# A two-block transformer kernel on one core: ordering the same instructions by a simulated timeline instead of the scheduler's default rule

## Chip, cores and metric

The kernel runs on one core of a Trainium2 chip. The metric is the device time of one execution in microseconds (us); lower is better. TensorE multiplies matrices, VectorE (DVE), ScalarE (ACT) and GpSimd (POOL) do the elementwise work, SyncE (SP) issues most of the transfers. Each of them works through its own queue of instructions and waits for others by semaphores.

## The reference

Two transformer blocks of 256 tokens with a model width of 1024 run behind one another, all in float32.

```python
def first_block(x, ...):
    h = x
    h = h + moba_attention(rms_norm(h, norm_mix[0]), ...)
    h = h + conv_ffn(rms_norm(h, norm_ffn[0]), ...)
    h = h + rwkv7_time_mix(rms_norm(h, norm_mix[1]), ...)
    h = h + conv_ffn(rms_norm(h, norm_ffn[1]), ...)
    return rms_norm(h, norm_final)

def second_block(x, mem, ...):
    mem_k, mem_v = jnp.split(mem @ mem_w_kv, 2, axis=-1)
    for i in range(2):
        mix = differential_attention(h, ...) if i == 0 else dsa_sparse_mla(h, ...)
        h = layer_norm(alpha * h + mix, ...)
        h = layer_norm(alpha * h + memory_cross_attention(h, mem_k, mem_v, ...), ...)
        h = layer_norm(alpha * h + hierarchical_moe(h, ...), ...)
    return h
```

The listing is shortened: the loop over the layers of the first block is written out, and arguments are left out. The time mix is a linear recurrence over the tokens with a state of 64 x 64 per head (16 heads). The sparse attention scores all keys with a small indexer, keeps the 64 best of each query (top-k) and attends to those alone. The layer of experts has 16 experts of width 512 and gives each token to two of them.

## The kernel before, in words

The stages run one after the other, in the order of `build`: moba attention, feed-forward, time mix, feed-forward, then twice an attention (differential, then sparse), memory attention and experts. Tokens stand in two tiles of 128. Activations are transposed (`to_T`, matmuls with an identity at L246) so that features lie on the partitions. A weight is loaded as float32 over SP's queue (`load`, L170) and split into a high and a low part: `wh` is a cast on ACT (L191), `wl = w - wh` a subtraction on VectorE, in places on POOL (L192). A product is then three matmuls, high by high, low by high and high by low (`mm3`, L215 to L217).

Two PSUM pools hold results: one of four tiles for short-lived products (`mm`, `pp`) and one of four for running sums (`acc`); some stages open further ones (`rkp`, `va`). A stage's instructions are recorded in program order, with some stages recorded as interleaved pieces: while the time mix works on its chunks, pieces of the memory projection (the tile `va`, keys and values of the memory attention) are recorded between its steps.

After the recording, the framework's scheduler puts each engine's instructions into the queue that the engine will work through. It keeps the data dependencies, hands out the buffers of the pools, and where several instructions of one engine could come next, its rule decides. No transfer, tile size, engine or pool is set there: only the order, and with it which buffer of a pool a tile gets. It is set up at L2005, by the `TileContext` around `build`.

The lines that the prediction's steps speak of:

- Norms: L276 adds the sums to the residual, L277 squares on ACT, L279 is a power on POOL, L282 the scaled rows on VectorE, L246 their transposes on TensorE. L352 to L369 are the layer norm.
- Moba attention: L475 and L476 scores of a head, L494 the scaled softmax on VectorE, L504 its transposes, L509 and L510 the product with the values.
- Time mix, mixes: L637 computes the mixed inputs on VectorE, L641 and L642 split them. L1161 to L1184 compute rotation angles for the second block on VectorE; they are independent of the time mix.
- Time mix, heads: the receptance and key projections write `rkp`; L730, L756, L770, L773, L790 and L801 prepare a group of four heads.
- Time mix, recurrence: L848 to L881 invert small triangular matrices, L911 to L966 run the chunks of 64 tokens: L929 reads the state `S`, L933 adds on VectorE, L940 gives `UV`, L952 and L958 the new state, L966 the output. Each chunk needs the state of the chunk before. L987 to L1013 normalise the output and transpose it (L1009); the output projection (`acc`) needs that.
- Sparse attention: L1834 and L1835 are the indexer's scores, one head of 16 at a time; L1837 a relu on ACT, L1841 and L1843 their weighted sum on VectorE. The top-k is a serial chain on VectorE: eight rounds of maximum and replacement (L1849, L1850). L1866 and L1874 project keys and values, L1884 are the attention scores, L1885 to L1893 the softmax, which needs the top-k's mask, L1736 its transposes, L1906 and L1907 the product with the values.
- Experts: L1612 and L1614 gather tokens, L1639 the gate and up products, L1645 the gated product on VectorE, L1654 its transposes, L1668 the down product, L1625 scatters the result back.

The top-k chain and its input, in the code:

```python
for rd in range(8):
    for t, cs in ((0, slice(0, 128)), (1, slice(128, 384))):
        vec.max(mx[:, t], sc[:, cs])
        vec.match_replace(sc[:, cs], mx[:, t], sc[:, cs], low)
```

Of the kernel before, what the change touches and what calls it, by code (L numbers as in the profile page):

```python
# [53 lines left out]


class MoeQueue:
    """Weight chunks of a memory attention and a MoE layer in the order of use: slots of a ring, and some filled only once."""

    def __init__(self, nc, wq, wo, wg, wu, wd):
        self.nc, self.ring, self.free, self.loaded, self.used = nc, [], [], [], 0  # L60
# [1948 lines left out]
```

## Time and profile before

| | before |
|---|---|
| median of three runs | 1748.44 us (1744.04, 1748.44, 1748.51) |
| span of the profiled execution | 1741.2 us |
| mean granted clock of TensorE | 0.958 of full speed |
| TensorE busy | 1619.0 us, 93% |
| VectorE busy | 888.9 us, 51% |
| ScalarE busy | 699.2 us, 40% |
| GpSimd busy | 186.8 us, 11% |
| data moved | 375.39 MB, 216 GB/s on average |

The span reaches from the first to the last instruction of one profiled execution; no other time of that execution is given. A run's time lies some microseconds above it. A busy share is an average over stages with different limits, so the prediction reads single stages. In the timeline the stages lie as follows (us from the start of the span): moba attention 0 to 147, feed-forward to 341, time mix to 650 (its mixes 350 to 397, its heads to 485), feed-forward to 845, differential attention to 970, memory attention to 1046, experts to 1297, sparse attention to 1406, memory attention to 1480, experts to the end.

A row of a timeline gives the start, the duration, the engine, the line, the operation with what it writes and reads, and how many such instructions stand in a row; a bracket gives the idle time before and what ended it. Matmuls are pipelined, so their durations overlap and the distance of two starts is the pace.

### The profile page before, as it was taken

What the parts mean: (1) busy time and instruction counts of PE and PEld (TensorE: products, weight loads), DVE (VectorE), ACT (ScalarE), POOL (GpSimd) and SP (SyncE); (2) the same over time, 40 slices, a digit from 0 to 9 for tenths busy, and PEclk for the clock granted to TensorE, in tenths of its full rate; (3) what the DMA queues carried; (4) which work ended last, traced back from release to release, by engine and by line L of the source; (5) the groups of instructions that cost most, each with busy time, mean ns of one, the idle gap of its engine ahead of it and who ended that gap; (6) DMA issues with size and microseconds to landing.
All of it is one profiled execution on the core that took longest, in us unless ns stands there. A gap on an engine that the chain in (4) does not pass through costs nothing. (4 is left out here: it accounts for less than half of the span.)

```text
span 1741.2 us, 26063 instructions
## 1 busy us (share of the span) xinstructions
PE 1619.0 (93%) x10383; PEld 1213.0 (70%) x10383; DVE 888.9 (51%) x1864; ACT 699.2 (40%) x1288; POOL 186.8 (11%) x153
## 2 busy tenths in 40 slices
PE   7899999879899999999999899999979989999995
PEld 6778999758788778999887785444427778544532
DVE  3567655498857567665568643111126964311112
ACT  5676455345434546554467432010116643201101
POOL 4610000056623110000101000000000000000000
PEclk9999999989969998999999899999989999999998
DMA  9324653432321329643661948999948177899983
GB/s 346 134 97 148 216 187 129 125 106 85 97 69 58 108 81 308 206 159 121 226 233 49 339 173 330 387 387 387 386 146 284 74 254 258 325 387 386 387 321 127
DMA packets 230353, 375.39 MB, mean 216 GB/s; under 512 B 17092, under 2 KB 105932, under 8 KB 230220
## 3 DMA queue, kind: packets, MB, share of 16 engines
q1 hardware_dynamic: 215616, 359.88, 58.7%
q10 hardware_dynamic: 14604, 13.71, 2.6%
q8 instruction: 86, 1.41, 0.3%
q14 instruction: 47, 0.39, 0.1%
HBM read 372.52 MB, written 1.05 MB: 215 GB/s over the span
## 5 line engine op out<-in xcount | busy, mean ns | idle before, releaser
L191 ACT CAST wh<-w 128x1024 fp32r<-128x1024 f32 (+1 forms) x253 | 260.3, 1039 | 232.5 <-PE mm L216 123.1
L192 DVE TENSOR_TENSOR wl<-w,wh 128x1024 fp32r<-128x1024 f32 (+1 forms) x214 | 257.1, 1210 | 151.9 <-ACT wh L191 151.4
L1639 PE MATMUL mm<-mw,xg 128*64 128x512 f32 x1024 | 230.2, 594 | 0.0
L217 PE MATMUL mm<-xh,wl 128*128 128x256 f32 x800 | 227.1, 284 | 0.0
L216 PE MATMUL mm<-xl,wh 128*128 128x256 f32 x800 | 226.9, 284 | 0.0
L215 PE MATMUL mm<-xh,wh 128*128 128x256 f32 x800 | 226.6, 283 | 0.0
L1639 PEld LDWEIGHTS mm<-mw,xg 128*64 128x64 f32 x1024 | 73.7, 137 | 144.0 <-issue 142.5
L215 PEld LDWEIGHTS mm<-xh,wh 128*128 128x128 f32 x800 | 151.9, 190 | 1.9
L216 PEld LDWEIGHTS mm<-xl,wh 128*128 128x128 f32 x800 | 151.3, 189 | 2.3 <-DVE xl L252 0.3
L217 PEld LDWEIGHTS mm<-xh,wl 128*128 128x128 f32 x800 | 151.5, 189 | 0.0
L1668 PE MATMUL mm<-mw,hT 128*64 128x512 f32 x512 | 118.7, 596 | 1.7 <-issue 1.7
L215 PE MATMUL acc<-wh,xh 128*128 128x512 f32 x284 | 112.9, 403 | 1.6 <-ACT xh L249 0.9
L216 PE MATMUL acc<-wl,xh 128*128 128x512 f32 x284 | 114.0, 402 | 0.0
L217 PE MATMUL acc<-wh,xl 128*128 128x512 f32 x284 | 113.3, 401 | 0.0
L192 POOL TENSOR_TENSOR wl<-w,wh 128x1024 fp32r<-128x1024 f32 x39 | 93.4, 2404 | 79.4 <-ACT wh L191 73.9
L1645 DVE TENSOR_TENSOR hid<-hid,mm 128x512 f32<-128x512 f32 x16 | 11.0, 687 | 168.3 <-PE mm L1639 168.3
L1668 PEld LDWEIGHTS mm<-mw,hT 128*64 128x64 f32 x512 | 36.6, 137 | 69.2 <-issue 67.5
L1675 DVE SCALAR_TENSOR_TENSOR Y<-mm,cs,Y 128x512 fp32r<-128x512 f32 x32 | 24.0, 751 | 114.2 <-ACT Y L1674 114.2
L1674 ACT ACTIVATE Y<-mm,cs 128x512 fp32r<-128x512 f32 x32 | 22.0, 687 | 146.8 <-PE mm L1668 146.8
L215 PE MATMUL acc<-wh,fh 128*128 128x512 f32 x176 | 69.5, 395 | 0.0
L217 PE MATMUL acc<-wh,fl 128*128 128x512 f32 x176 | 69.5, 396 | 0.0
L216 PE MATMUL acc<-wl,fh 128*128 128x512 f32 x176 | 69.3, 394 | 0.0
(529 smaller groups left out, 3127.8 us busy)
## 6 DMA issues: line engine op xcount, KB each, us to landing
mw<-in_moe_w_gate_dram SPq DMA_DIRECT2D x61, 1024.0 KB, 14.2
mw<-in_moe_w_up_dram SPq DMA_DIRECT2D x60, 1024.0 KB, 14.3
mw<-in_moe_w_down_dram SPq DMA_DIRECT2D x57, 1024.0 KB, 14.1
w<-in_ffn_w_gate_dram SPq DMA_DIRECT2D x22, 1024.0 KB, 5.9
w<-in_ffn_w_up_dram SPq DMA_DIRECT2D x22, 1024.0 KB, 6.7
w<-in_ffn_w_down_dram SPq DMA_DIRECT2D x22, 1024.0 KB, 6.3
w<-in_attn_w_qkv_dram SPq DMA_DIRECT2D x12, 1024.0 KB, 10.8
w<-in_a_w_in_dram SPq DMA_DIRECT2D x12, 1024.0 KB, 10.6
```

The costliest lines, as they stand in the source:

```text
L191: nc.scalar.copy(r[0], raw)
L192: (lo_eng or nc.vector).tensor_tensor(r[1], raw, r[0], op=ALU.subtract)
L215: mm(out, lhs[0], rhs[0], start=start, stop=False)
L216: mm(out, lhs[0], rhs[1], start=False, stop=False)
L217: mm(out, lhs[1], rhs[0], start=False, stop=stop)
L1639: mm(ps[64 * e:64 * e + 64], xg[:, k, e * 64:e * 64 + 64], mq.slab(w[2 * (k // 4) + e], k % 4), start=k == 0, stop=k == 7)
L1645: tt(hid, hid, gu[1], op=ALU.mult)
L1668: mm(pd[hf][64 * e:64 * e + 64], hT[:, k, 64 * e:64 * e + 64], mq.slab(w[2 * hf + e], k), start=k == 0, stop=k == 3)
L1674: act.activation(y[0], pd[hf], AF.Copy, scale=cs)
L1675: vec.scalar_tensor_tensor(y[1], pd[hf], cs, y[0], op0=ALU.mult, op1=ALU.subtract)
```

## The change

```diff
@@ kernel(**inputs)
     out = nc.dram_tensor("out_0_dram", (1, S, D), F32, kind="ExternalOutput").ap()
-    with tile.TileContext(nc) as tc:
+    with tile.TileContext(nc, schedule_with_timeline_sim=True) as tc:
         build(tc, aps, out[0])
```

The framework's scheduler orders the instructions by a timeline that it simulates instead of by its default rule. A docstring of a class goes as well, which leaves the line numbers as they are. The instructions of each engine are the same ones; their order in each queue differs, and with it the assignment of buffers. In the two feed-forward layers the order on TensorE stays the same. Three places at which it differs:

POOL, at the start of the time mix (rms is the norm's scale, L192 the subtraction for a weight's low part, aT a constant that is cleared, xvl and xl low parts of the mixes). Before:

```order
L279 TENSOR_TENSOR rms<-rms,mhalf 128x1 x2
L824 MEMSET aT 128x256
L825 MEMSET aT 128x16
L279 TENSOR_TENSOR rms<-rms,mhalf 128x1 x2
L192 TENSOR_TENSOR wl<-w,wh 128x1024
L642 TENSOR_TENSOR xvl<-xm,xvh 128x256
L642 TENSOR_TENSOR xl<-xm,xh 128x256 x2
```

With the change:

```order
L279 TENSOR_TENSOR rms<-rms,mhalf 128x1 x2
L192 TENSOR_TENSOR wl<-w,wh 128x1024
L824 MEMSET aT 128x256
L279 TENSOR_TENSOR rms<-rms,mhalf 128x1
L825 MEMSET aT 128x16
L279 TENSOR_TENSOR rms<-rms,mhalf 128x1
L642 TENSOR_TENSOR xvl<-xm,xvh 128x256
L642 TENSOR_TENSOR xl<-xm,xh 128x256 x2
```

The subtraction moved ahead of the last two powers of the norm; before, it stood behind them.

TensorE, the end of the chunks' second half in the time mix (L929 reads the state, L940 makes UV, L966 the output, L1009 transposes the normalised output, va is the memory projection, acc the output projection). Before:

```order
L215 MATMUL va<-wh,xh 128x512
L216 MATMUL va<-wl,xh 128x512
L217 MATMUL va<-wh,xl 128x512
L940 MATMUL mm<-Z,A 64x64
L215 MATMUL va<-wh,xh 128x512
L1009 MATMUL mm<-c_ident,Y 128x128 x3
L940 MATMUL mm<-Z,A 64x64 x7
L1009 MATMUL mm<-c_ident,Y 128x128
L1013 MATMUL mm<-tg,g_5252 128x128 x4
L966 MATMUL mm<-UV,A 64x64 x8
L216 MATMUL va<-wl,xh 128x512
L217 MATMUL va<-wh,xl 128x512
```

With the change:

```order
L952 MATMUL mm<-UV,BK 64x64 x8
L966 MATMUL mm<-UV,A 64x64 x8
L929 MATMUL mm<-S,AR 128x64 x8
L940 MATMUL mm<-Z,A 64x64
L1009 MATMUL mm<-c_ident,Y 128x128 x4
L940 MATMUL mm<-Z,A 64x64 x7
L1013 MATMUL mm<-tg,g_5252 128x128 x4
L966 MATMUL mm<-UV,A 64x64 x8
L215 MATMUL acc<-wh,xh 128x512
L216 MATMUL acc<-wl,xh 128x512
L215 MATMUL acc<-wh,xh 128x512
L216 MATMUL acc<-wl,xh 128x512
```

The memory projections between the steps of the chain, and behind L966, have moved to places further ahead; behind L966 now twelve matmuls of the output projection stand before the next L1009.

TensorE, sparse attention, from the key projection (L1866) and the value projection (L1874) to the attention scores (L1884); before, all rows of L1834 and L1835 stand ahead of this piece. Before:

```order
L215 MATMUL acc<-cqh,wh 96x256
L216 MATMUL acc<-cql,wh 96x256
L217 MATMUL acc<-cqh,wl 96x256
L1866 MATMUL acc<-ckvT,w 96x256 x16
L1874 MATMUL acc<-w,ckvT 128x512 x8
L1884 MATMUL acc<-kT,qT 128x128
L1884 MATMUL acc<-kT,qT 128x256
```

With the change (the 16 matmuls of L1866 and five of the eight of L1874 stand ahead of this piece):

```order
L1834 MATMUL mm<-kiz,qiT 128x128
L1835 MATMUL mm<-kiz,qiT 128x256
L1834 MATMUL mm<-kiz,qiT 128x128
L1835 MATMUL mm<-kiz,qiT 128x256
L1874 MATMUL acc<-w,ckvT 128x512 x3
L1834 MATMUL mm<-kiz,qiT 128x128
L1835 MATMUL mm<-kiz,qiT 128x256
L1834 MATMUL mm<-kiz,qiT 128x128
L1835 MATMUL mm<-kiz,qiT 128x256
L1884 MATMUL acc<-kT,qT 128x128
L1884 MATMUL acc<-kT,qT 128x256
```

The indexer's scores moved back behind most of the projections, so that the last two heads of them stand directly ahead of L1884.

## Rows read from the trace of the kernel before

**Rows 1.** Page, busy time: busy us, share of the span, instructions.

```profile
PE 1619.0 (93%) x10383; PEld 1213.0 (70%) x10383; DVE 888.9 (51%) x1864; ACT 699.2 (40%) x1288; POOL 186.8 (11%) x153
```

**Rows 2.** TensorE's waits: line, released by; us in all, times, longest.

```profile
PE mm L246 <- DVE nrm L282: 20.2, 8, 9.2
...
PE mm L504 <- DVE s L494: 6.4, 3, 3.8
...
PE pp L801 <- DVE rn L758: 5.0, 3, 2.8
PE mm L1654 <- DVE hid L1645: 4.3, 7, 0.8
...
PE mm L929 <- DVE S L958: 2.5, 1, 2.5
```

**Rows 3.** TensorE's timeline, moba attention: start us, us, engine, line, work, count [idle before].

```profile
54.09 0.28 PE L216 MATMUL acc<-xl,wh 128*128 128x256 f32 x1
54.21 0.28 PE L217 MATMUL acc<-xh,wl 128*128 128x256 f32 x1
...
59.11 0.30 PE L504 MATMUL mm<-c_ident,s 128*128 128x128 f32 x1 [3.76 <-DVE s L494]
...
61.59 0.41 PE L216 MATMUL acc<-xl,wh 128*128 128x256 f32 x1
61.80 0.41 PE L217 MATMUL acc<-xh,wl 128*128 128x256 f32 x1
```

**Rows 4.** POOL's timeline at the start of the time mix.

```profile
353.74 2.63 POOL L192 TENSOR_TENSOR wl<-w,wh 128x1024 fp32r<-128x1024 f32 x1 [5.40 <-DMA vraw<-in_rwkv_w_rkv_dram]
```

**Rows 5.** Busy time by window, mixes of the time mix: window, its us, each engine's busy us.

```profile
348.24:391.77 43.53, 34.33 (x134) 22.73 (x134) 43.36 (x72) 17.78 (x34) 24.62 (x23) 0.90 0.35 106
```

**Rows 6.** VectorE's timeline, mixes of the time mix.

```profile
352.49 5.03 DVE L637 SCALAR_TENSOR_TENSOR xm<-xx,par,x 128x256 f32<-128x256 f32 x6
...
390.75 3.41 DVE L637 SCALAR_TENSOR_TENSOR xm<-xx,par,x 128x256 f32<-128x256 f32 x6
...
394.48 0.61 DVE L1173 TENSOR_SCALAR angk<-anga 128x48 f32<-128x48 f32 x1
...
398.46 0.21 DVE L1184 SCALAR_TENSOR_TENSOR anga<-angy,anga 128x48 f32<-128x48 f32 x1
```

**Rows 7.** TensorE's timeline, heads of the time mix.

```profile
473.46 0.90 PE L790 MATMUL mm<-c_ident,bk 128*128 128x128 f32 x3 [2.19 <-DVE bk L781]
```

**Rows 8.** Busy time by window of line L872: PE, PEld, granted clock, DMA share.

```profile
486.90:517.70 30.80, 3.82 (x64) 3.56 (x64) 0.50 0.19 59
575.70:600.00 24.30, 1.20 (x64) 1.09 (x64) 1.00 0.36 118
```

**Rows 9.** TensorE's timeline, chunks of the time mix, second half.

```profile
595.09 1.11 PE L929 MATMUL mm<-S,AR 64*128 64x64 f32 x16
...
617.88 1.15 PE L966 MATMUL mm<-UV,A 128*64 128x64 f32 x16
...
628.16 0.66 PE L1009 MATMUL mm<-c_ident,Y 128*128 128x128 f32 x4 [1.02 <-DVE Y L1004]
```

**Rows 10.** Busy time by window of tile va: first PE with its count.

```profile
595.00:614.00 19.00, 9.69 (x34) 5.80 (x35) 0.00 (x0) 1.17 (x2) 1.00 0.26 85
617.00:628.50 11.50, 5.63 (x23) 4.24 (x23) 0.00 (x0) 1.17 (x2) 1.00 0.32 97
```

**Rows 11.** TensorE's timeline, sparse attention.

```profile
1352.96 0.60 PE L1835 MATMUL mm<-kiz,qiT 128*128 128x256 f32 x2
...
1369.69 4.75 PE L1884 MATMUL acc<-kT,qT 128*128 128x128 f32 x28
1374.73 1.36 PE L1736 MATMUL mm<-c_ident,s 128*128 128x128 f32 x6 [0.29 <-DVE s L1893]
```

**Rows 12.** VectorE's timeline, sparse attention.

```profile
1360.81 0.61 DVE L1849 MAX8 mx<-sc 128x8 f32<-128x128 f32 x2
...
1374.39 0.55 DVE L1893 TENSOR_SCALAR s<-s,st 128x128 f32<-128x128 f32 x2
```

## The prediction

> **What bounds the kernel now.** I read the page's busy shares and slices first, then TensorE's waits, then the timelines of the places where the order changes. TensorE is busy for 1619.0 us of the span of 1741.2 [rows 1]: whatever an order can win or lose on this engine is idle time and clock. By the table of its waits, the largest are the norms between layers (L246 waits 20.2 us for the scaled rows of L282, in eight places), and behind them waits of matmuls that stand too early in the queue: L504 6.4 us in three, L801 5.0 in three, L929 2.5 in one, L1654 4.3 in seven [rows 2]. Each stops the whole engine, since the matmuls behind it in the queue, ready or not, come after it. The timeline shows it: the transposes L504 stand directly behind their own scores, TensorE stops for 3.76 us, and 1.1 us later it runs at the half clock; there a 256-column matmul starts every 0.21 us instead of every 0.12 [rows 3]. A stretch of 3.4 us at the half clock so costs about 3.4 x (1 - 0.12/0.21) = 1.5 us.
>
> The change has the same instructions on the same engines; only each engine's own order differs. So the rule of the sum is: a matmul moved back behind ready ones removes its wait; ready matmuls used up early are missing later, where a chain over VectorE has nothing beside it; and work moved ahead on VectorE or POOL delays what is behind it.
>
> **The change part by part.**
> 1. Moba attention (the stretch around [rows 3]): L475, L504 and L509 go behind 10 to 40 more projection matmuls. What that can remove is 6.4 us of waits [rows 2] and two half-clock stretches of 1.5 each, 9.4 in all. The projections used early are missing for the last heads, beside the output projection: one wait like the longest, 3.8 us, and a stretch of 1.5 come back. Bounds -9.4 and 0; I take **-4**.
> 2. Start of the time mix: on POOL the subtraction L192, 2.63 us [rows 4], now stands ahead of both L279, the powers of the rms norm, for which TensorE's transposes wait. On SP, one weight load (L170) goes ahead of loads of the value projection, on ACT two casts (L191) ahead of the squares (L277). TensorE has nothing else there. Bounds 0 (the weight is there before the norm begins) and +5 (the load as well is late); **+2.6**, the subtraction itself.
> 3. Mixes of the time mix: VectorE is busy 43.36 of 43.53 us [rows 5], so its work is the path. The rope angles (L1161 to L1184, thirteen instructions, which stand behind the last mix L637 and take from 394.48 to 398.46 [rows 6]) are pulled in between the mixes. Bounds 0 and +3.9; **+2**. The same rows show a reverse effect: six mixes take 5.03 us while that POOL subtraction runs, and 3.41 later [rows 4, 6]; since it moves ahead, up to 1.6 us could come back here, and that lies in the bounds. The Trainium skill (page "SBUF — State Buffer", section on the two separate sides) says that VectorE with two SBUF inputs and GpSimd lock each other out of a shared port for a whole instruction. By that rule all of the 1.6 comes back and this sum would be 1.6 lower; the trace agrees in direction (5.03 against 3.41), though shorter POOL operations run beside the later mixes too.
> 4. Heads of the time mix (rkp projections between L730 and L801): L756, L770, L790 and L801 go behind 10 to 20 more projections. Waits of 5.0 for L801 [rows 2] and 2.2 for L790 [rows 7], with three half-clock stretches of 1.5, make 11.7. The matmuls brought forward are missing for the last heads. Bounds -11.7 and 0; half of it, **-6**.
> 5. Inverses and chunks: memory projections (va) fill the inverses early, which takes the 2.5 of L929 away and lets the clock return sooner. In the half-clock stretch 64 matmuls of L872 took 3.82 us, and 1.20 at the full clock later [rows 8]; that is 2.6 for L872, of which I take 2. But the second half's chain, from L929 at 595.09 to L966 at 617.88 and on to L1009 at 628.16 [rows 9], loses its filler: 34 va matmuls, 9.69 us, ran between 595 and 614, and 23, 5.63 us, between 617 and 628.5 [rows 10], seven acc matmuls with them. Now none stand in the chain, and 12 acc in the last gap. If the chain's steps were only held up by the filler, the loss is 0; if the latencies of VectorE are what counts, 9.7. I take 5. In the last gap 18 fewer at 5.63/23 = 0.245 leave 4.4. Together -2.5 - 2 + 5 + 4.4 = **+5** (bounds -9 to +12).
> 6. Sparse attention, the dearest term: in the order before, all sixteen indexer scores (L1834, L1835) are done by 1353.5, and VectorE's top-k (from L1849 at 1360.81 to the first normalised probabilities L1893 at 1374.39, 13.6 us [rows 12]) runs beside the projections of keys and values; TensorE then waits 0.29 [rows 11]. In the new order the last two scores stand behind those projections, directly ahead of L1884. Only 4.75 us of L1884 [rows 11] are left to lie beside 13.6 us. That leaves 13.6 - 4.75 - 0.3 = 8.5, and 1.5 of half clock behind it: **+10**. Bounds: 0 if TensorE gets to L1834 late for other reasons, +12 with two stretches.
> 7. The rest. Differential attention: its scores start behind about 40 more matmuls and the tail is shorter, 0 to +2, **+1**. Norms: VectorE now does the second tile's additions ahead of the first tile's scale, at seven of the boundaries; 20.2 us in eight places [rows 2] is 2.5 each, and I take 0.4 each, **+3** (0 to +6). Experts: scatter and gather matmuls (L1625, L1612) move ahead of L1654 into waits of 4.3 [rows 2]: **-3** (-4.3 to 0). In both feed-forward layers the order stays, 0.
>
> Sum: -4 + 2.6 + 2 - 6 + 5 + 10 + 1 + 3 - 3 = +10.6. The median shown is 1748.44, 7.2 above the profiled span; that part does not depend on the order. **1748.4 + 10.6 = 1759.**
>
> **The rivals.**
> - Faster: the matmul queue does not run dry. Where matmuls are moved back, the waits go in full (moba 5.4 more, heads 5.7 more), and the chunk chain, no longer held up by fillers, becomes shorter, so its 5 is 0. For it: half of the chain's 19 us was filler [rows 10]. Against: the same matmuls are only spent once. 10.6 - 16.1 = -5.5: **1743**, or less if a tail is covered too. It decides at the chain: L929 to the next L929 under about 6.5 us without a TensorE wait.
> - No change: gains as in the sum, but the top-k and the chunk tail are half covered by output projections that the new order has near (-5 and -5). +0.6: **1749**. That the change does little is a part of this: both feed-forward layers keep their order.
> - Much slower: every new wait is followed by the half clock for two stretches (3 us, in three places 9), and the heads' gain is eaten because the last heads stand alone (6). 10.6 + 15 = +26: **1774**.
>
> **How the numbers follow.** My forecast (about 1752 to 1768 by its own terms) has 0.42; faster 0.20; no change 0.18; much slower 0.20. A measurement of this kernel tells about 0.3%, 5.2 us, from no change; so faster 0.20, same 0.18, slower 0.42 + 0.20 = 0.62. The range leaves out the outer half of each outer rival: 1738 to 1781, wide since the terms 4, 5 and 6 each have bounds some ten apart.
>
> **What would show it.** In the profile of the changed kernel: L504 and L801 gone from TensorE's waits, or small; a wait of 8 to 10 us at the first L1736 behind L1884, released by VectorE's L1893; waits of several us at L1009, L940 and L952 in the second chain; L246 behind L282 longer where the time mix starts; L1654's waits gone. The prediction is wrong if the top-k still lies beside matmuls, if the chunk chain shows no idle time, or if the waits of moba and heads turn up again under another line.

## The result, and the profile after

The changed kernel takes 1792.11 us (median of four runs, 1789.71 to 1792.76) against 1748.47 for the kernel before, run beside it. The ratio is 1.0258, with a 95% interval of 1.0233 to 1.0284: **slower by 2.6%**. The sign was forecast; the size, 1759, was not, and the time lies above the range.

The page of the changed kernel, the line that answers to [rows 1]; its span is 1787.8 us:

```profile
PE 1615.0 (90%) x10383; PEld 1222.0 (68%) x10383; DVE 891.1 (50%) x1864; ACT 700.3 (39%) x1288; POOL 186.3 (10%) x153
```

The work is the same: 1615.0 us of TensorE instead of 1619.0. By the page's count all of the loss is idle time of that engine, 122.2 us before (1741.2 - 1619.0) and 172.8 now. TensorE's waits in the changed kernel, to be read against [rows 2] (line, released by; us in all, times, longest):

```profile
PE mm L246 <- DVE nrm L282: 26.9, 8, 9.3
...
PE mm L790 <- DVE bk L781: 13.3, 5, 9.4
PE acc L1884 <- DVE s L1885: 9.6, 1, 9.6
...
PE mm L790 <- ACT eL L741: 5.9, 1, 5.9
PE mm L246 <- DVE h L282: 5.1, 1, 5.1
PE mm L929 <- DVE S L958: 4.3, 2, 3.0
...
PE mm L606 <- DMA prow<-in_rwkv_r_k_dram: 3.6, 1, 3.6
...
PE mm L1009 <- DVE Y L1004: 3.5, 1, 3.5
...
PE mm L1654 <- DVE hid L1645: 1.6, 2, 0.8
...
PE mm L504 <- DVE s L494: 0.4, 1, 0.4
```

What was to go has gone: L504 from 6.4 to 0.4, L1654 from 4.3 to 1.6, and L801, 5.0 before, is no longer listed. What has come is larger: L790 has 13.3 here and a further 5.9 behind ACT (2.4 before), L1884 9.6, the norms' L246 more than before.

By stages, each from the end of TensorE's last matmul of the stage before to the end of its own last (us, profiled executions; "again" is a second profile of the kernel before, E16; E13 and E14 are told of below; the changes are taken before rounding):

| stage | before | again | changed | change | E13 | E14 |
|---|---|---|---|---|---|---|
| moba attention | 147.4 | 147.7 | 151.4 | +4.1 | 146.0 | 147.3 |
| both feed-forwards | 388.9 | 389.0 | 390.6 | +1.7 | 390.9 | 390.2 |
| start of the time mix | 9.1 | 10.2 | 14.9 | +5.8 | 11.9 | 12.1 |
| mixes | 48.0 | 48.0 | 49.6 | +1.6 | 49.3 | 48.0 |
| heads | 86.8 | 86.4 | 98.8 | +12.0 | 98.8 | 87.7 |
| inverses and chunks | 165.2 | 164.4 | 171.8 | +6.6 | 174.4 | 162.2 |
| differential attention | 124.3 | 124.3 | 134.6 | +10.3 | 135.0 | 124.3 |
| both memory attentions | 150.9 | 150.2 | 156.3 | +5.3 | 158.0 | 150.2 |
| both expert layers | 499.1 | 501.5 | 488.5 | -10.6 | 489.5 | 490.0 |
| sparse attention with its projections | 109.9 | 108.4 | 119.5 | +9.6 | 120.6 | 108.8 |

The column of changes sums, with 0.3 at the tail, to 46.7; the spans differ by 46.6. The stages of the kernel before repeat within 1.5 us from one profile to the next, an expert layer within 2.6; inverses and chunks of one unchanged order spread from 171.8 to 175.4 us between the runs below, at granted clocks of 0.87 to 0.84.

**The heads**, the largest loss. TensorE's timeline of the changed kernel (start, us, engine, line, work, count [idle before]):

```profile
474.21 0.61 PE L770 MATMUL pp<-c_ident,rx 128*128 128x128 f32 x4
474.65 0.51 PE L773 MATMUL pp<-rkb,rk 128*128 128x2 f32 x4
475.02 0.59 PE L756 MATMUL pp<-blk,sq 128*128 128x2 f32 x4
...
485.35 1.12 PE L790 MATMUL mm<-c_ident,bk 128*128 128x128 f32 x4 [9.41 <-DVE bk L781]
```

VectorE's, in the same gap:

```profile
475.34 2.50 DVE L821 TENSOR_SCALAR aT<-ginv,pm 128x256 f32<-128x256 f32 x1
477.87 1.37 DVE L822 SCALAR_TENSOR_TENSOR aT<-ginv,pm,aT 128x256 f32<-128x256 f32 x1
...
480.67 0.42 DVE L774 TENSOR_TENSOR kk<-kk,pp 128x256 f32<-128x256 f32 x1
...
482.76 2.54 DVE L781 SCALAR_TENSOR_TENSOR bk<-aa,eN 128x256 f32<-128x256 f32 x1
```

L790 transposes `bk`, which VectorE makes (L774, L777, L781) from what L773 has just written. Before, projections of `rkp` stand between L773 and L790, and TensorE idles 2.19 us [rows 7]. Now these projections run from 468.21 on, ahead of both, and only two of them are left behind L756. L790 has moved back, as the prediction says, and its producer has moved back with it. On VectorE, steps of the inverse (L821, L822) stand ahead of L774 as well.

**Sparse attention**, TensorE of the changed kernel:

```profile
1406.82 0.60 PE L1835 MATMUL mm<-kiz,qiT 128*128 128x256 f32 x2
1407.26 2.78 PE L1884 MATMUL acc<-kT,qT 128*128 128x128 f32 x16
1419.66 4.21 PE L1884 MATMUL acc<-kT,qT 128*128 128x128 f32 x12 [9.62 <-DVE s L1885]
```

The last indexer score ends directly ahead of L1884, as read from the order. The wait of 9.6 us comes inside L1884, when its four buffers are full, and not at L1736 behind it.

**The chunks**, second half; the wait stands where [rows 9] have 1.02:

```profile
666.88 0.64 PE L1009 MATMUL mm<-c_ident,Y 128*128 128x128 f32 x4 [3.49 <-DVE Y L1004]
```

**The start of the time mix.** POOL's timeline answers to [rows 4], and now shows the powers behind the subtraction:

```profile
353.33 2.45 POOL L192 TENSOR_TENSOR wl<-w,wh 128x1024 fp32r<-128x1024 f32 x1 [202.56 <-DMA a<-in_rwkv_a_dram]
...
356.00 0.54 POOL L279 TENSOR_TENSOR rms<-rms,mhalf 128x1 f32<-128x1 f32 x1
```

But ACT shows something that no step of the prediction has. Its queue issues the small constants `prow` (ACTq rows); the changed kernel:

```profile
341.83 0.30 ACTq L602 DMA_DIRECT2D prow<-in_rwkv_w_dram  x1
...
345.67 0.28 ACTq L602 DMA_DIRECT2D prow<-in_rwkv_k_k_dram  x1
...
348.94 0.28 ACTq L603 DMA_DIRECT2D prow<-in_rwkv_r_k_dram  x1
...
351.26 1.04 ACT L191 CAST wh<-w 128x1024 fp32r<-128x1024 f32 x1 [12.90 <-PE mm L606]
...
353.16 0.63 ACT L277 ACTIVATE nrm<-h 128x512 f32<-128x512 f32 x1
```

The kernel before:

```profile
336.27 0.30 ACTq L602 DMA_DIRECT2D prow<-in_rwkv_w_dram  x1
...
337.46 0.28 ACTq L602 DMA_DIRECT2D prow<-in_rwkv_k_k_dram  x1
...
339.20 0.31 ACTq L603 DMA_DIRECT2D prow<-in_rwkv_r_k_dram  x1
...
342.94 0.63 ACT L277 ACTIVATE nrm<-h 128x512 f32<-128x512 f32 x1 [9.93 <-DMA prow<-in_rwkv_k_a_dram]
```

Five 4-KB transfers are stretched over 7.1 us instead of 2.9, the last of them goes out 2.5 us behind the beginning of this stage (348.94 - 346.45) instead of 2.2 us ahead of it (341.37 - 339.20), and ACT, in whose queue they stand, comes to the squares of the norm only behind them. A likely reason stands in the program that is built: a transfer signals its end on one of eight semaphores, which are handed out in turn over SP's and ACT's 456 transfers together (57 on each, in the traces), in the order in which the scheduler places them. So the order decides not only which buffer a tile gets, as the text on the kernel before says, but also which semaphore a transfer gets. A transfer waits in its queue until the one before it on its semaphore has landed. Before, `r_k` (L603) follows a load of ACT's own (L592, issued at 331.2); in the changed kernel it follows a 512-KB weight on SP that is issued from 337.2 to 339.3, and `k_k` follows another. Whether this is the cause was tried in E13 and E14.

### The profile page after: what moved, and what is told of

The parts are those of the page before. It is cut to its first block, busy times and chain, and to the rows that moved or that the text cites. A ratio compares the mean times of both kernels' runs of the same rounds, so it can differ in the third digit from the quotient of the medians.

```text
span 1787.8 us, 26087 instructions
## 1 busy us (share of the span) xinstructions
PE 1615.0 (90%) x10383; PEld 1222.0 (68%) x10383; DVE 891.1 (50%) x1864; ACT 700.3 (39%) x1288; POOL 186.3 (10%) x153
## 5 line engine op out<-in xcount | busy, mean ns | idle before, releaser
L192 DVE TENSOR_TENSOR wl<-w,wh 128x1024 fp32r<-128x1024 f32 (+1 forms) x214 | 258.6, 1222 | 186.5 <-ACT wh L191 185.5
L1639 PE MATMUL mm<-mw,xg 128*64 128x512 f32 x1024 | 226.3, 593 | 0.0
L215 PEld LDWEIGHTS mm<-xh,wh 128*128 128x128 f32 x800 | 151.9, 190 | 4.9 <-issue 3.0
L192 POOL TENSOR_TENSOR wl<-w,wh 128x1024 fp32r<-128x1024 f32 x39 | 93.2, 2396 | 296.2 <-DMA a<-in_rwkv_a_dram 202.6
L1668 PE MATMUL mm<-mw,hT 128*64 128x512 f32 x512 | 114.4, 595 | 1.7 <-issue 1.7
L217 PE MATMUL acc<-wh,xl 128*128 128x512 f32 x284 | 104.7, 402 | 0.0
L1674 ACT ACTIVATE Y<-mm,cs 128x512 fp32r<-128x512 f32 x32 | 22.0, 688 | 143.2 <-PE mm L1668 132.9
L215 PEld LDWEIGHTS acc<-wh,xh 128*128 128x128 f32 x284 | 54.1, 193 | 27.8 <-ACT wh L191 4.7
## 6 DMA issues: line engine op xcount, KB each, us to landing
w<-in_attn_w_qkv_dram SPq DMA_DIRECT2D x12, 1024.0 KB, 10.6
```

The costliest lines, as they stand in the source:

```text
L192: (lo_eng or nc.vector).tensor_tensor(r[1], raw, r[0], op=ALU.subtract)
L215: mm(out, lhs[0], rhs[0], start=start, stop=False)
L217: mm(out, lhs[1], rhs[0], start=False, stop=stop)
L1639: mm(ps[64 * e:64 * e + 64], xg[:, k, e * 64:e * 64 + 64], mq.slab(w[2 * (k // 4) + e], k % 4), start=k == 0, stop=k == 7)
L1668: mm(pd[hf][64 * e:64 * e + 64], hT[:, k, 64 * e:64 * e + 64], mq.slab(w[2 * hf + e], k), start=k == 0, stop=k == 3)
L1674: act.activation(y[0], pd[hf], AF.Copy, scale=cs)
```

## The experiments

In nearly all of them an order is pinned: a table lists instructions of a queue in the order that they have in the other kernel, and each gets a dependency on the one before it that orders the schedule and makes no wait. Everything else is ordered by the kernel's own rule, which can place instructions of unpinned stages and engines elsewhere than in the changed kernel; where that matters, the number of moved instructions is given (the fewest that have to be moved to turn one order into the other, counted in the traces). E1 to E8, E10 to E12 and E16 are single runs. They stand beside runs of the kernel before of 1742.71 (E1 to E4), 1746.2 (E5 to E8), 1744.72 (E9 to E12) and 1744.65 (E13 to E16); by the ratio of 1.0258 the changed kernel lies some 45 us above them. The edit that E2 to E14 share, in short form (some of them call it one line earlier in the order of stages, behind the time mix):

```diff
-                            x = b.memattn(h, x or b.test_x(h), li, ...)
+                            x = b.memattn(h, x or b.test_x(h), li, ...); pin(b.nc, tc, PINS)
...
+def pin(nc, tc, table):
+    at = {i.name: i for i in nc.cur_bb.bb.instructions}
+    for row in table:
+        last = None
+        for ins in (at[n] for n in names(row) if n in at):
+            if last is not None:
+                tc.add_manual_dep(ins, last.name, DependencyInfo(NoSync, DATA), reason="pin")
+            last = ins
```

### E1: the sparse attention, indexer scores first

```diff
-            mm(p[:, 128:384], qiT[:, hd // 2, 128:256], kiz[:, hd % 2], start=True, stop=True)
+            ix = mm(p[:, 128:384], qiT[:, hd // 2, 128:256], kiz[:, hd % 2], start=True, stop=True)
...
-        for n in range(0, 8, 2):
-            k_of(n)
...
+        with tc.issue_after(ix.ins):
+            for n in range(0, 8, 2):
+                k_of(n)
...
```

Key and value projections are issued behind the last indexer score.

> The timeline's order with one rule added: the key and value projections (L1866, L1874) queue behind the last indexer score (L1835). Theory (top-k uncovered because the last scores stand behind the projections): the 9.6 us wait of L1884 behind L1885 goes, sparse attention falls from 79.9 us to about 70, the span from 1787.8 to about 1778. Rival (the scores are late anyway, since ScalarE's relus and VectorE's sums hold them back): the wait only moves to L1834 or L1866, the stage falls by under 3 us.

Measured: 1791.24 us. TensorE's timeline:

```profile
1415.71 4.75 PE L1884 MATMUL acc<-kT,qT 128*128 128x128 f32 x28
1421.75 0.70 PE L1736 MATMUL mm<-c_ident,s 128*128 128x128 f32 x3 [1.29 <-DVE s L1893]
```

The wait of 9.6 us is gone and the stage is 3.2 us shorter (76.7 instead of 79.9), not 10: its idle time falls from 11.0 to 6.1, since other waits come in its place, among them 3.1 us of L1834 behind ACT's relu L1837. The time of the whole kernel shows no gain. The position of the scores causes the wait; it isn't all that makes the stage slow.

### E7: the whole order of the sparse attention as before

```diff
+PINS = [all five queues, sparse attention]
```

> The timeline's order, with the sparse attention (1297 to 1406 us of before) held in the order of before on all five queues. Theory (in the run with the scores first, the relus L1837 that ScalarE's queue still had behind casts and copies, and VectorE's sums behind subtractions, kept the rest of the loss): the stage from L246 on falls from 79.9 us to 70 to 71, against 76.7 with TensorE's order alone; the span about 1778. Rival (the later start of its weights' loads on SP is what is left): 75 or more.

Measured: 1780.35 us, the stage 69.5 instead of 79.9 (69.9 before). So the +10.0 is the order of this stage alone. What E1 didn't give back lies for the most part with the other queues: E10 below has TensorE's whole order of before in this stage, and takes 77.6.

### E2, E3, E4: the heads, TensorE's order, VectorE's, and all

```diff
+PINS = [E2: TensorE, heads; E3: VectorE, heads; E4: all five queues, heads]
```

> The timeline's order, with only TensorE's instructions of the time mix's heads held in the order of before. Theory A (the projections that stood between a producer L773 and its consumer L790 have moved ahead of both): the waits of L790, 19.2 us in six, fall under 6; heads fall from 98.8 us to 88 to 90. Rival B (VectorE's own order: steps of the triangular inverse, L821 to L830, ahead of L774): the waits stay above 12 us under L790 or another line, heads stay above 95.

> The timeline's order, with only VectorE's instructions of the heads held in the order of before. Theory A (TensorE's order): L790 still waits more than 12 us, heads stay above 95. Rival B (VectorE's order): its waits fall under 8, heads come to 87 to 91.

> The timeline's order, with the heads' instructions of all five queues held in the order of before. Both theories: heads back to 86 to 89 us (98.8 with the change), the span near 1776. If the heads stay above 93, the cause lies ahead of them: the weights' loads and casts, or the state in which the mixes leave the engines.

Measured: E2 1786.55, heads 83.0 us, chunks 183.6. E3 1803.63, heads 104.0, chunks 179.9. E4 1782.57, heads 86.8, chunks 179.3. With TensorE's order of before (E2), L790's waits are gone and the heads are short again. E3 fits neither expectation. L790's waits fall from 19.2 us in all (13.3 + 5.9) to 6.2, so the steps of the inverse ahead of L774 on VectorE have a part in them, but L801 waits instead and the heads get longer:

```profile
PE pp L801 <- DVE rn L758: 12.3, 5, 4.6
...
PE mm L790 <- DVE bk L781: 6.2, 6, 3.0
```

The two are no clean split, since the rule orders the engine that isn't pinned anew: against the changed kernel, 45 of VectorE's 159 instructions of the heads have moved in E2, and 68 of TensorE's 608 matmuls there in E3. That TensorE's order is enough to bring the heads back is shown; that VectorE's order plays no part is not.

The next stage takes most of the gain back: heads and chunks together are 270.6 in the changed kernel, 266.6 in E2, 266.1 in E4, 252.0 before. Waits aren't the reason. Inverses and chunks in the changed kernel (window, its us, each engine's busy us and count, granted clock),

```profile
509.77:681.60 171.83, 154.20 (x1814) 133.85 (x1814) 94.38 (x168) 71.44 (x116) 28.14 (x20) 0.87 0.22 70
```

in E2:

```profile
492.58:676.15 183.57, 165.69 (x1844) 144.42 (x1844) 100.41 (x173) 71.61 (x117) 29.72 (x21) 0.81 0.22 70
```

and in E3:

```profile
513.35:693.28 179.93, 162.32 (x1845) 141.79 (x1844) 96.52 (x171) 71.30 (x116) 28.12 (x20) 0.83 0.21 66
```

TensorE is idle for 17.6, 17.9 and 17.6 us; what differs is the granted clock, 0.87, 0.81 and 0.83 (0.82 in E4), and with it TensorE's busy time. In E2 and E4 the order of this stage isn't the changed kernel's either: of its 1844 matmuls 449 and 226 have moved, but only 12 in E3. Why the clock is lower isn't shown.

### E5, E6: the chunks, and the whole time mix

```diff
+PINS = [E5: all five queues, inverses and chunks; E6: all five queues, the time mix from its start]
```

> The timeline's order, with the inverses and chunks of the time mix (486 to 650 us of before) held in the order of before on all five queues; heads as with the change. Theory (memory projections spent early leave the second chain bare): idle time of that stage 17.6 us back to about 7, the stage from 171.8 to about 163, the span about 1779. Rival (the heads and the chunks share one loss, the filler that waits of the heads draw in): the stage stays over 169, or the heads get longer by what it gains.

> The timeline's order, with the whole time mix (341 to 650 us of before: norm, mixes, heads, chunks) held in the order of before on all five queues. Theory: the stage returns from 335.1 us to 309 to 311, the span to about 1763; the rest of the loss stays where it was. Rival (what comes in, buffers and loads left by the feed-forward layer, costs as well): over 316.

Measured: E5 1786.63, heads 98.8 as in the changed kernel, chunks 166.7 (about 163 expected) with 7.4 us of idle TensorE instead of 17.6. E6 1770.73. Its time mix, from the start on, is this window:

```profile
347.16:658.31 311.15, 278.59 (x2628) 233.34 (x2626) 222.98 (x435) 139.06 (x242) 115.39 (x89) 0.88 0.30 90
```

It takes 311.2 us instead of the changed kernel's 335.1 (309.2 before), which has 58.1 us of idle TensorE (335.15 - 277.10) where E6 has 32.6:

```profile
346.45:681.60 335.15, 277.10 (x2628) 233.49 (x2626) 223.54 (x434) 138.97 (x241) 113.21 (x89) 0.87 0.28 84
```

The 20 us of mixes, heads and chunks are their order, and have to be undone together. The start stays at 13.9, though each queue there has the order of before.

### E8: the norms

```diff
+PINS = [all five queues, a window around each of eight norms]
```

> The timeline's order, with 9 to 24 us around each of eight norms at the boundaries of layers held in the order of before on all five queues. Theory (the second tile's additions and weight casts stand ahead of the first tile's scale): TensorE's waits of L246 at the norms, 60 us in all with the change and 43 before, return to 43 to 47; the span falls by 12 to 16, to 1772 to 1776. Rival (the norms wait for last sums that TensorE delivers late, which these windows do not move): the waits stay over 54, the span falls by under 5.

Measured: 1785.11. L246 behind the norms waits 50.2 us instead of 60.1 (43.4 before):

```profile
PE mm L246 <- DVE nrm L282: 29.1, 8, 9.3
...
PE mm L246 <- DVE h L369: 14.1, 4, 5.8
...
PE mm L246 <- DVE h L405: 7.0, 1, 7.0
```

The memory attentions lose their 5 us (73.2 and 74.3 instead of 78.2 and 78.0); the start of the time mix gets longer, 16.9. So 10 us of waits go, and 4.6 us of the span (1783.2 instead of 1787.8): in the waits between the two expectations, in the span at the rival's.

### E10, E11: TensorE's order, or the others'

```diff
+PINS = [E10: TensorE; E11: the other four; both in moba, time mix, differential and sparse attention]
```

> The timeline's order, with TensorE alone held in the order of before in moba attention, time mix, differential and sparse attention. Theory (the matmul order is the larger cause in heads, chunks and sparse attention; VectorE, ScalarE and POOL are it at the norms and in moba attention): heads and chunks together 254 to 260 us (270.6 with the change, 252.1 before), sparse attention 76 to 77, moba attention stays over 150, norm and start of the time mix stay over 13. Rival (the other engines' order is the cause everywhere): under a quarter of the loss comes back in any stage.

> The timeline's order, with VectorE, ScalarE, POOL and SP held in the order of before in the same four stages, and TensorE free. Theory: heads and chunks stay over 265 us, sparse attention over 75, moba attention returns to 147 to 149, the differential attention from 134.6 to 127 to 130. Rival: heads and chunks under 258.

Measured: E10 1777.79, E11 1803.08. Heads and chunks: 257.7 and 271.5 (270.6 changed, 252.0 before). Differential attention: 125.7 and 132.9 (134.6, 124.3). Sparse attention: 77.6 and 74.3 (79.9, 69.9). With TensorE in the order of before, most of the loss of heads, chunks and differential attention goes, but only 2.3 of the 10.0 us of the sparse attention. Much of that is lost elsewhere: the first memory attention takes 84.9 and 85.8 us (78.2 changed, 76.9 before), and moba attention, which E11 was to bring back to 147 to 149, 154.6 and 161.9. Of E11's expectations only that for heads and chunks came true.

E11 isn't "TensorE in the changed order": under the pins of the others the rule orders TensorE anew, and against the changed kernel 525 of the 1844 matmuls of the inverses and chunks and 156 of the 608 of the heads have moved. So the pair shows what TensorE's order of before is worth, and not what the other four queues are worth.

### E12: moba, the differential attention and the start

```diff
+PINS = [all five queues; moba, start of the time mix, differential attention]
```

> The timeline's order, with moba attention, the last 28 us ahead of the time mix's mixes (its parameter loads among them), and the differential attention with the norms on both its sides held in the order of before on all five queues. Theory: moba attention 151.4 back to 147 to 148, the norm and start of the time mix 14.9 to 9 to 10, differential attention 134.6 to 124 to 125; the span falls by 17 to 20, to 1768 to 1771. Rival (the parameter loads of L602 and L603 wait for memory that the feed-forward layer frees): the start stays over 13, the rest as in the theory.

Measured: 1794.03, where 1768 to 1771 were expected for the span. The differential attention is back at 124.3, so its 10 us are its order; but the memory attention behind it takes 83.8 instead of 78.2. And moba takes 151.9 and the start 17.3, though each queue there has the order of before. Something else than the order of the queues makes these two long.

### E9: the order of before everywhere but in the experts

```diff
+PINS = [all five queues, everything up to the experts, in both layers]
```

> The timeline's order in the two layers of experts alone (and the last norm); everything else (0 to 1046 and 1297 to 1480 us of before) held in the order of before on all five queues. Theory: the experts keep their gain of 3 to 7 us each, nothing else changes, so the kernel is 6 to 11 us faster than before, a ratio of 0.994 to 0.996. Rival (the experts' shorter times with the change were work that the stages ahead had taken over): within 2 us of before.

Measured: 1745.74 us (median of 12 runs) against 1744.72 (17 runs), ratio 1.000, interval 0.9986 to 1.0014. So the whole loss lies outside the experts. Yet the gain of the experts, 1.4 and 5.3 us here, is missing in the total: moba takes 154.3 and the start 13.3, against 147.4 and 9.1. Of the transfers, 59 of the 315 up to the first experts have another completion semaphore than before; `r_k` follows a 512-KB weight of SP's on its semaphore, as in the changed kernel, and so it does in E12.

### E13: the changed kernel with other completion semaphores

```diff
+PINS = [all five queues as the change orders them;
+        SP's and ACT's transfers as one chain, merged as before for the constants of moba and time mix]
```

The order of each of the five queues is that of the change, but for four rope loads and the constants beside them, which change places among themselves; 28 transfers get another semaphore.

> The changed kernel with the order of every queue left as it is (four rope loads and the constants beside them in another sequence among themselves); only the interleaving of SP's transfers with ACT's is that of before for the first dozen constants and for the time mix's constants, so that 28 transfers get another of the eight completion semaphores. Theory (a transfer waits for the one before it on its semaphore, and in the changed kernel the constants of the time mix stand behind 512-KB weights): r_k (L603) is issued before 344 us instead of 348.94, the transpose L606 waits under 1.5 us instead of 3.6, the start of the time mix takes 12 to 13 us instead of 14.9, the first stage 148 to 150 instead of 151.4; in all 1785 to 1789. Rival (the start hangs on the vector and POOL queues alone): 14 to 15 us and 151 to 152 again, 1791 to 1793.

Measured: 1785.98 us (median of four runs), ratio to the kernel before 1.0222, interval 1.0205 to 1.0239; the change itself has 1.0258 (1.0233 to 1.0284). The two intervals still touch, so the gain is read from the stages. ACT at the start of the time mix:

```profile
335.03 0.30 ACTq L602 DMA_DIRECT2D prow<-in_rwkv_w_dram  x1
...
340.26 0.28 ACTq L603 DMA_DIRECT2D prow<-in_rwkv_r_k_dram  x1
...
342.88 1.04 ACT L191 CAST wh<-w 128x1024 fp32r<-128x1024 f32 x1 [10.19 <-DMA prow<-in_rwkv_r_k_dram]
```

In E13, as in the kernel before, `r_k` follows ACT's own load (L592) on its semaphore. It is out 0.8 us ahead of TensorE's last matmul of the feed-forward (341.05), L606 waits 1.8 us instead of 3.6, and the start takes 11.9 instead of 14.9. Moba takes 146.0 instead of 151.4. E1 to E7 repeat the changed kernel in both places: moba 151.2 to 152.4, and the start, whose order E1 to E5 and E7 leave alone, 13.1 to 13.7. So all of moba's loss comes from the semaphores; of the start's 5.8 us it is 1.2 to 3.0, as one takes these runs or the changed kernel's own profile. Moba in the changed kernel shows the same on ACT:

```profile
11.46 0.35 ACTq L430 DMA_DIRECT2D msk<-in_causal_dram  x1
11.85 0.59 ACT L249 CAST xh<-mm 128x512 fp32r<-128x512 f32 x1 [1.36 <-DMA sin<-in_rope_sin_dram]
```

and in E13:

```profile
8.73 0.41 ACTq L430 DMA_DIRECT2D msk<-in_causal_dram  x1
...
10.48 0.59 ACT L249 CAST xh<-mm 128x512 fp32r<-128x512 f32 x1 [0.51 <-PE mm L246]
```

### E14: E9 with the semaphores of before

```diff
 PINS = [all five queues, everything up to the experts, in both layers;
+        SP's and ACT's transfers up to the first experts as one chain, merged as before]
```

> The kernel of e9 (the order of before everywhere but in the two expert stages), now with the interleaving of SP's and ACT's transfers of before as well, so that each transfer up to the first experts has the completion semaphore that it had in before. Theory (the semaphores explain what e9 lost in moba and at the start of the time mix): moba 147 to 149 us instead of e9's 154.3, the start 9 to 11 instead of 13.3, the experts keep their gain; ratio 0.994 to 0.997. Rival (these stages differ from one profiled execution to the next, whatever the semaphores): moba anywhere from 147 to 154, ratio 0.999 to 1.001 as e9.

Measured: **1731.72 us** (median of five runs, 1731.09 to 1734.5), ratio 0.9922, interval 0.9909 to 0.9936; 0.8% faster than the kernel before, and faster than the changed one. Moba is 147.3 again, the first memory attention 76.9 instead of E9's 79.5. The start, 12.1, comes back only in part: `r_k` is issued at 341.51, 1.0 us ahead of the stage's beginning, where the kernel before issues it 2.2 ahead. TensorE's waits:

```profile
PE pp L801 <- DVE rn L758: 6.5, 3, 3.5
PE mm L504 <- DVE s L494: 6.4, 3, 3.8
```

The waits of before are all there; what is left of the change is its order in the experts. E9 and E14 have the same order on four queues, and on SP's but for four pairs of expert weights that change places; otherwise they differ in the semaphores alone, and their intervals lie far apart. Of the 14.8 us between the two profiled executions moba has 7.0, the first memory attention 2.6, and the first layer of experts 2.8. Inverses and chunks have 5.3, at nearly the same idle time (7.2 and 6.9 us) and a granted clock of 0.86 and 0.88; that this too comes from the semaphores is not shown. Other stages take 2.9 back.

### E15: the experts' order put into the kernel before

```diff
+                            pin(nc, tc, PINS)
                             with tc.If(over > 64):
...
+PINS = [all five queues as the change orders them, the two expert layers]
```

> The kernel before, with its own rule, semaphores and order everywhere but in the two expert stages, which take the changed kernel's order. Theory (the experts' order alone is worth what the stages show, 3.4 and 7.2 us at most): moba 147 to 149, start 9 to 10, experts 246 to 247 and 242 to 244; ratio 0.994 to 0.997. Rival (what the experts gain is the clock's, and comes with the execution, not with the order): experts 248 to 250 in both, ratio 0.999 to 1.001.

Measured: 1737.33 us (median of five runs), ratio 0.9959, interval 0.9945 to 0.9973. The experts' order is worth 7 us by itself, though the profiled execution shows little of it in their stages (249.5 and 247.6, the rival's numbers); where the 7 us lie isn't shown. Why E14 gains nearly twice as much stays open: its order in the experts is nearly the same (12 matmuls of TensorE and 31 instructions of VectorE have moved), its semaphores there differ.

### E16: the kernel before once more, without an edit

> The kernel before, unchanged, profiled a second time, to see how far the stages of one program differ between executions. If they repeat, moba is 147 to 148 us, the start of the time mix 9 to 10, the first memory attention 76 to 78, the experts 249 to 251. If moba comes out over 150 or the start over 11, the losses of e9 in these stages are no effect of its program.

Measured: 1743.69 us; the stages stand in the table above ("again"). They repeat, so what E9 and E12 lose in moba and at the start belongs to their programs.

## Why the prediction was right and wrong

The steps against the stages; the sum was +10.6, the spans differ by 46.6.

1. Moba, -4: measured +4.1. L504's waits went as said. With the semaphores of before (E13) the stage is 1.4 shorter than before, inside the bounds. What failed is that the step looks only at the five queues: the semaphores cost 5.4 (151.4 - 146.0).
2. Start of the time mix, +2.6: measured +5.8, of which 1.2 to 3.0 are the semaphores (E13). The rest, 2.8 to 4.6, may be the subtraction ahead of the powers (2.45 us in the changed kernel), but that isn't shown: E14, with POOL's order of before, takes 12.1 as well.
3. Mixes, +2: measured +1.6. VectorE's 48 mixes L637 took 28.4 us in all before and 27.7 now, so 0.7 came back of the 1.6 that the rows beside POOL's subtraction held. The one mix of 2.58 us, which ran beside the subtraction L192, is gone; but 16 mixes instead of 14 take about 0.95 us instead of 0.47, each of them beside one of POOL's shorter subtractions L642. What did not hold is that "all of the 1.6 comes back": the step counts the one long subtraction and not the short ones. The Trainium skill (page "SBUF — State Buffer", section on the two separate sides) has VectorE with two SBUF inputs and GpSimd lock each other out of a shared port for a whole instruction. The trace agrees in direction, with 2.58 us beside L192 and 0.95 beside L642 against 0.47; but mixes of 0.47 us lie beside L642 too (13 of 32 in the changed kernel).
4. Heads, **-6: measured +12.0. This is the step that failed**, 18 of the 36 us. It says that L756, L770, L790 and L801 "go behind 10 to 20 more projections", and takes waits away for it. What counts is how much work stands between a matmul and the one that produces its input, not how far it moves: L773 moved back too, the filler between it and L790 went, and the wait grew from 2.19 to 9.4. With TensorE's order of before the waits of L790 are gone (E2, heads 83.0); VectorE's order has a part in them too (E3). The order showed where the filler went; it was read for one line at a time.
5. Inverses and chunks, +5: measured +6.6. The waits named (L1009, L940, L952, L929) are the ones that came; TensorE's idle time there rose from 7.1 to 17.6. The mechanism was right, the size nearly. How much the granted clock weighs here was not in the step: at 17.6 us of idle time the stage takes 171.8 us at 0.87 in the changed kernel and 179.9 at 0.83 in E3.
6. Sparse attention, **+10: measured +10.0** (79.9 against 69.9). The wait came as described, one line away from where it was put: the buffers of the scores fill first, so it stands in L1884. That the size fits is in part luck. The step puts all 10 us on TensorE's queue, but the scores in front give back 3.2 of them (E1) and TensorE's whole order of before 2.3 (E10); all 10 need the other queues as well (E7).
7. Differential attention, +1: measured +10.3; sized from the scores and the tail alone. TensorE now waits 5.1 us for L282 at its beginning, and its tail has a row of waits under 1.2 us; E10 and E12 show that the order does it, though in both the memory attention behind it gets 5.6 to 6.7 longer. Norms, +3: the memory attentions alone lost 5.3, undersized. Experts, -3: -10.6 in the stages, -7.3 by E15. Feed-forwards, 0: +1.7, with nearly the same order on TensorE (7 of 1331 matmuls in the first and 26 of 1325 in the second have moved).

Of the rivals, the much slower one came nearest: the heads' gain eaten, and the half clock behind each new wait. Windows (us, busy us of PE and the others, then the granted clock) of heads and sparse attention in the changed kernel,

```profile
410.97:509.77 98.80, 75.84 (x638) 70.52 (x637) 73.62 (x143) 38.88 (x69) 55.51 (x40) 0.90 0.32 94
...
1376.24:1456.18 79.94, 68.98 (x342) 54.10 (x340) 51.94 (x172) 41.04 (x101) 0.20 (x1) 0.94 0.25 87
```

and in the kernel before:

```profile
398.50:485.30 86.80, 77.52 (x611) 70.54 (x609) 73.70 (x160) 38.96 (x71) 53.27 (x40) 0.94 0.33 98
...
1336.60:1406.50 69.90, 67.67 (x350) 53.37 (x349) 54.91 (x183) 43.11 (x106) 0.76 (x2) 1.00 0.27 94
```

The granted clock falls from 0.94 to 0.90 and from 1.00 to 0.94. The rival priced the half clock at 9 us in all; by the page's count the loss is idle time (50.6 us more), and what the clock costs beside it isn't separated. The 7.2 us between span and median that the sum carried along belonged mostly to the one profiled execution: in E9, E13 and E14 the profiled run is 1.9 us above its span.

## What to carry to other kernels

When an order changes, read for each matmul what stands between it and its producer on the same engine, and what its producer's engine does meanwhile; a line that moves back together with its producer has gained nothing. Before a later stage of an experiment is read, compare its order too: a pin in one stage lets the rule order the next one anew. Undo a scheduler's order stage by stage and keep what pays: here 1731.72 us came from the new order in one kind of layer, and the old one, with the old semaphores, elsewhere. After pinning an order, compare the transfers' semaphores as well as the queues.

## What was not expected of the hardware and the program

The same instructions in the same order on each queue don't make the same time. E9 and E14 differ by 14 us (1745.74 and 1731.72), and, but for four pairs of loads on SP, only in which of eight completion semaphores a transfer shares with which other. A 4-KB constant on ACT's queue went out 2.5 us behind the end of the feed-forward (348.94 - 346.45) where it followed a 512-KB weight of SP's queue on its semaphore, and 0.8 us ahead of it (341.05 - 340.26, E13) where it followed a load of ACT's own; ACT's own arithmetic stood behind it.

At the same idle time of TensorE a stage can differ by 8 us with the granted clock: inverses and chunks took 171.8 us at 0.87 in the changed kernel and 179.9 at 0.83 in E3, where 12 of their 1844 matmuls had moved.
